# Second half's output projection moved 15 pairs into the first half's last FFN, with seven products behind it

## The chip, the cores and the metric

The kernel runs on one core of one Trainium2 chip. The metric is the device time of one execution in microseconds; the time given for a kernel is the median of several runs. A profile is one further execution, taken by the hardware profiler. The engines are called TensorE (PE; its weight loads PEld), VectorE (DVE), ScalarE (ACT), GpSimd (POOL) and SyncE (SP, which here issues nearly all transfers).

## The reference, cut to what matters

One layer of a hybrid decoder, 1024 channels wide, for a prompt of 1024 tokens and 8 single tokens that continue older sequences, all in float32:

```python
x = x + 0.5 * swiglu_ffn(rms_norm(x, ffn1_norm), w_gate1, w_up1, w_down1)   # first FFN, 2816 hidden
h = rms_norm(x, mix_norm);  proj = h @ w_in
ya = silu(layer_norm(causal_dwconv(glu(proj), width 31)))                   # mixer, group A
ys = grouped_rms_norm((ssd_scan(causal_dwconv(proj, width 4)) + D * xs) * silu(z))   # mixer, group B
x = x + concat([ya, ys]) @ w_out                                            # output projection
x = x + 0.5 * swiglu_ffn(rms_norm(x, ffn2_norm), w_gate2, w_up2, w_down2)   # last FFN
y = rms_norm(x, final_norm)
# swiglu_ffn(x) = (silu(x @ w_gate) * (x @ w_up)) @ w_down
```

The outputs are `y` for the prompt and the 8 tokens, and the new states of the two convolutions and of the scan.

## The kernel before

**Halves.** The tokens are cut in two: half 0 has the first 512 prompt tokens and the 8 single ones (520 columns, in two blocks of 260), half 1 the other 512. Activations lie with channels on the partitions, as 8 tiles per 1024 channels. State `sa` belongs to half 0, `sb` to half 1.

**Precision.** Every float32 operand is split in `hi` (rounded by a ScalarE copy) and `lo` (the rest, by a VectorE subtraction); weights likewise in `wh`/`wl` from the raw tile `wr`. A product is three matmuls: `wh` by `hi`, `wh` by `lo`, `wl` by `hi` (`mm3`, L348).

**Units.** TensorE's work is a list `prog` of units (`Unit`, L50), each one weight tile and its matmuls; on half 0 each matmul has 260 columns, on half 1 512. A *pair* is one of the 22 hidden tiles of an FFN: `gate(f)` and `up(f)`, 48 matmuls each on half 0. `down(gi, d)` multiplies the hidden tiles of group `gi` into output tile `d`: 3 matmuls per hidden tile and block. `GROUPS` (6, 5, 5, 6) and `GROUPS7` (3, 4, 4, 4, 3, 4) say how the 22 are grouped.

**Seven products.** `sevens()` computes a pair in seven smaller products, as Strassen's scheme in the Winograd form does with a 2 x 2 split: 7 x 12 matmuls of half the tokens (260 columns on half 0, 256 on half 1) in place of gate and up. Its weights are sums of quarter tiles (`ws`, four VectorE instructions per pair), each split by ScalarE and VectorE (`ww`), and its activations sums of token halves (`t12`, `t34`), made by `norm7` together with the norm. Before the change the first FFN of half 0 (`f1a`) has 3 plain pairs and 19 in seven products, the last FFN of half 0 (`f2a`) 22 plain pairs, the last FFN of half 1 (`f2b`) 22 in seven products, and the first FFN of half 1 (`f1b`) 22 plain pairs. With `hold` some last groups' downs are kept until all products are done.

**Order.** The program on TensorE is: `f1a`; four units of `f1b`; input projection of half 0; rest of `f1b`, under which half 0's mixer runs on VectorE, ScalarE and partly TensorE; output projection of half 0 (16 units); input projection of half 1; `f2a`, under which half 1's mixer runs; output projection of half 1 (`wout_units`, after all 22 pairs); the last 8 downs of `f2a`, under which `late_norm_b` makes half 1's statistics, norm and sums; `f2b`. The final norm of half 0 (`final_task`) is started after the last down of `f2a` has been issued.

**Planner.** The order of VectorE's and ScalarE's instructions is worked out when the kernel is built. Side work (mixer, norms) is written as generators in `Runner`, and a model clock with a price per instruction (`cost_t` for TensorE, L191) says when an operand will be ready; a step is emitted when its engine can take it. Urgent tasks go first. Evictions (`post`) are emitted with their unit. If a unit is not `ready`, the clock is moved on in steps of 0.1 us and side work is emitted until it is. Each engine runs its own instructions in the order in which they were emitted; transfers go through SP's queue in order too. Work tiles come from one pool of 70 slots.

**Rows of x.** `rms_task` stores the residual rows in DRAM (`xsp`) and `reload` brings them back when the next stage adds to them. Half 1's rows after its output projection stay in SBUF (`sb.x`) until the last FFN adds to them.

Of the kernel before, what the change touches and what calls it, by code (L numbers as in the profile page):

```python
# [5 lines left out]
F32 = mybir.dt.float32  # L6
# [184 lines left out]
def cost_t(op, aps, k):  # L191
    if op == "transpose":
        return 0.11
    n = size(aps[0])
    if aps[1].dtype == F32R:
        return 0.003 + 0.000417 * n
    return 0.00167 * max(n, 128) * (0.64 if aps[1].shape[-1] == HD else 1.0)


# [5 lines left out]
def body(tc, xt0, xt1, vec, tri, eye, hexp, wgu1, wgu2,  # L205
# [124 lines left out]
    def split(t, h, n=None):  # L330
        n = n or NTOK[h]
        hi = slot(n, F32R, "hi")
        lo = slot(n, F32R, "lo")
        S.activation(out=hi, in_=t[:, :n], func=AF.Copy)
        clk.defer(V, [t, hi], lo, lambda: V.tensor_tensor(out=lo, in0=t[:, :n], in1=hi.bitcast(F32), op=ALU.subtract))
        return hi, lo
# [82 lines left out]
    def rms_task(st, h, gname, spill=None):  # L419

        rs = slot(NTOK[h], nm="rs")
        yield from rstd_task(st.acc, NTOK[h], D_, rs)
        yield from norm_task(st, h, gname, rs, spill)

    def norm_task(st, h, gname, rs, spill=None):
        n = NTOK[h]
        hn = []
        last = None
        for k in range(KT + 1):
            if k < KT:  # L430
                yield need(V, st.x[k], rs)
                t = slot(n, nm="hn")
                V.scalar_tensor_tensor(out=t, in0=st.x[k][:, :n], scalar=vv(gname, k), in1=rs, op0=ALU.mult, op1=ALU.mult)
                if spill:
                    store(spill[k], st.x[k][:, :n])
                st.x[k] = None
            if last is not None:
# [5 lines left out]
    def norm7(st, h, gname, rs, whole):  # L443


        n = NTOK[h]
        m = n // 2
        st.hn7, st.read, tt = [None] * KT, [], []
        for k in range(KT // 2):
            ts = []  # L450
            for j in (k, k + KT // 2):
                yield need(V, st.x[j], rs)
                t = slot(n, nm="hn")
                V.scalar_tensor_tensor(out=t, in0=st.x[j][:, :n], scalar=vv(gname, j), in1=rs, op0=ALU.mult, op1=ALU.mult)
                st.read.append(j)
                yield need(S, t)
                st.hn7[j] = split(t, h, n if whole or j > k else m)
                ts.append(t)
            up, dn = ts
            a, b = slot(n, nm="t12"), slot(n, nm="t34")  # L460
            yield need(V, up, dn)
            V.tensor_tensor(out=a[:, :m], in0=up[:, m:], in1=up[:, :m], op=ALU.subtract)
            V.tensor_tensor(out=b[:, :m], in0=dn[:, m:], in1=up[:, m:], op=ALU.subtract)
            yield need(V, a)
            V.tensor_tensor(out=a[:, m:], in0=dn[:, m:], in1=a[:, :m], op=ALU.subtract)
            yield need(V, a)
            V.tensor_tensor(out=b[:, m:], in0=dn[:, :m], in1=a[:, m:], op=ALU.subtract)
            both = []
            for t in (a, b):
                yield need(S, t)  # L470
                both.append(split(t, h))
            tt.append(both)
            del ts, up, dn, a, b, t
        st.tt = tt

    def reload(st, h, src, d):
# [9 lines left out]
    def always():  # L486
        return True

    def ffn_units(h, st, wgu, wd, late_norm=False, rows=None, last=None, plain=None, hold=1):


        groups = GROUPS if plain is None else GROUPS7
        starts = [sum(groups[:g]) for g in range(len(groups))]

        def ready():
# [206 lines left out]
        if plain is not None:  # L702
            for f in range(plain):
                out += [gate(f), up(f)]
                if f + 1 in starts:
                    out += [down(starts.index(f + 1) - 1, d) for k in range(KT // 2) for d in (k, k + KT // 2)]
            more, held = sevens()
            out += more
            st.seven_end = len(out)
            out += held  # L710
            if last:
                return out + [end(d, b) for b in range(2) for d in range(KT)]
            return out + [down(len(groups) - 1, d) for d in range(KT)]
# [122 lines left out]
        out += [zu(i) for i in range(KT)]  # L836
        return out

    def wout_units(h, st, mx):
        n = NTOK[h]  # L840
        cur = {}

        def unit(d, j):
            def go(w):
                if j == 0:
                    reload(st, h, xsp[h], d)
                cur["p"] = mmt(h)
# [426 lines left out]
    def mix_tasks(h, mx, other):  # L1274
# [155 lines left out]
    mx = [State(), State()]  # L1430
    for m in mx:
        m.u, m.xs, m.xn, m.z, m.dtT = [], [None] * 12, 0, 0, None
        m.dt_done = m.ssd_done = m.sample_done = m.gate_done = m.ya_ready = m.ys_ready = False
# [12 lines left out]
    def late_norm_b():  # L1446
        rs = slot(NTOK[1], nm="rs")
        yield from rstd_task(sb.acc, NTOK[1], D_, rs)
        yield from norm7(sb, 1, "ffn2_norm", rs, False)

    def start_norm(st, h, g):
        return act(lambda: run.add([rms_task(st, h, g, spill=xsp[h])], True))

    def first_stat_b():

# [28 lines left out]
    prog += [start_norm(sa, 0, "ffn2_norm"), act(lambda: run.add(mix_tasks(1, mx[1], sa)))] + win_units(1, sb, mx[1])  # L1484
    prog += f2a[:-8] + wout_units(1, sb, mx[1])
    prog += [act(lambda: run.add([late_norm_b()], True))] + f2a[-8:]
    prog += [act(lambda: run.add([final_task(sa, sa.acc, yt0, 0, NTOK[0])]))] + f2b
    units = [u for u in prog if isinstance(u, Unit)]

    with tc.manual_schedule():  # L1490
# [37 lines left out]
        def first_norm():  # L1528
            yield from rstd_task(sa.acc, n, D_, sa.rs)
            sa.late = False  # L1530
            yield from constants()
            yield from norm7(sa, 0, "ffn1_norm", sa.rs, False)
        run.add([first_norm()], True)
        i, made = 0, 1
        for u in prog:
# [44 lines left out]
SLOTS = 70  # L1580
LEAD = 4
STAT_B = 80
RAWS = 4
TAIL = 256
SAMPLE_LATE = True
# [90 lines left out]
```

## Time and profile before

| | |
|---|---|
| median of 3 runs | 2196.7 us (2195.86 to 2197.72) |
| the profiled execution | 2199.06 us, of which 2197.3 are the span from the first to the last instruction |
| mean granted TensorE clock | 0.989 |
| TensorE busy | 2148.5 us, 14711 matmuls |
| VectorE busy | 1710.4 us |
| ScalarE busy | 947.9 us |
| moved by DMA | 255.17 MB |

The profiled execution's own time is 2.4 us above the median of the runs. Times inside the trace are microseconds from the start of the span. In tile names the number of the buffer is left out, so `mm<-hi,ww` is every matmul of a seven-product pair's rounded parts. All instructions bear the line of one helper (L162), so work is told apart by its tiles. A number in square brackets is the idle time of the engine in front of the instruction and what ended it. Matmuls are pipelined, so the time of one is longer than the step from one to the next.

### The profile page before, as it was taken

To read this page: it belongs to the slowest core of one execution; us is meant where nothing else is said; L and a number is where in the kernel's file an instruction comes from. 1 tells how busy PE (TensorE), PEld (TensorE's weight loads), DVE (VectorE), ACT (ScalarE), POOL (GpSimd) and SP (SyncE) were. 2 spreads that over 40 slices of the span, in tenths; PEclk is the share of its full clock that TensorE was granted. 3 is DMA by queue.
4 is the path that set the end of the run, shared out by engine and by line. 5 is a ranking of instruction groups with operands and counts; after the bars stand their busy time and mean duration, and the time that the engine had idled before them with its cause. 6 is when DMAs were issued, how large, how long until landed. Compare 5 with 4: busy or idle time off the path is not lost.

```text
span 2197.3 us, 36877 instructions
## 1 busy us (share of the span) xinstructions
PE 2148.5 (98%) x14711; PEld 1974.9 (90%) x14711; DVE 1710.4 (78%) x3010; ACT 947.9 (43%) x1679; POOL 2.4 (0%) x24
## 2 busy tenths in 40 slices
PE   8999999999999999999999999999999997999997
PEld 7899999999987788889987889999999897899997
DVE  7877788699999899966489998988534368777776
ACT  5544454424556422453233556533423234544452
POOL 0000000000000000000000000000000000000000
PEclk9999999999999999999999999999999998999998
DMA  4323334423344455425243553442233323333322
GB/s 133 95 97 125 103 108 141 149 79 105 102 154 152 124 171 180 154 77 183 89 134 81 96 161 118 129 149 87 82 110 114 103 82 101 90 114 96 105 90 81
DMA packets 107987, 255.17 MB, mean 116 GB/s; under 512 B 14312, under 2 KB 30600, under 8 KB 107816
## 3 DMA queue, kind: packets, MB, share of 16 engines
q1 hardware_dynamic: 107240, 252.30, 38.0%
q8 instruction: 115, 1.88, 0.3%
q10 hardware_dynamic: 576, 0.52, 0.1%
q14 instruction: 56, 0.46, 0.1%
HBM read 231.90 MB, written 20.88 MB: 115 GB/s over the span
## 4 chain that ended last, share of the span: by engine, by line
PE 76%; DVE 4%; DMA 0%; issue 0%; ACT 0%; DVEq 0%
PE mm L162 73%; PE aux L162 4%; DVE x L162 1%; DVE ws L162 1%; DVE ww L162 1%; DMA zr<-zsp 0%; DVE lo L162 0%; DVE wl L162 0%; DVE acc L162 0%; DVE t L162 0%; DVE xc L162 0%; DVE ra L162 0%; DVE hn L162 0%; DVE ya L162 0%; DVE ry L162 0%
## 5 line engine op out<-in xcount | busy, mean ns | idle before, releaser
L162 PE MATMUL mm<-hi,wh 128*128 128x260 f32 (+2 forms) x3146 | 862.0, 326 | 7.1 <-ACT wh L162 6.5
L162 PE MATMUL mm<-lo,wh 128*128 128x260 f32 (+2 forms) x3146 | 850.7, 322 | 2.6 <-DVE lo L162 2.3
L162 PE MATMUL mm<-hi,wl 128*128 128x260 f32 (+2 forms) x3146 | 849.1, 322 | 0.5 <-DVE wl L162 0.5
L162 PEld LDWEIGHTS mm<-hi,wh 128*128 128x128 f32 x3146 | 526.7, 189 | 60.1 <-ACT wh L162 6.5
L162 PEld LDWEIGHTS mm<-lo,wh 128*128 128x128 f32 x3146 | 525.1, 189 | 51.5 <-DVE lo L162 4.6
L162 PEld LDWEIGHTS mm<-hi,wl 128*128 128x128 f32 x3146 | 525.1, 189 | 48.3 <-DVE wl L162 0.7
L162 DVE TENSOR_TENSOR wl<-wr,wh 128x1024 fp32r<-128x1024 f32 (+4 forms) x359 | 359.7, 1004 | 126.1 <-ACT wh L162 124.8
L162 PE MATMUL mm<-hi,ww 128*128 128x256 f32 (+1 forms) x2296 | 425.6, 285 | 13.2 <-ACT hi L162 7.9
L162 ACT ACTIVATE wh<-wr 128x1024 fp32r<-128x1024 f32 (+4 forms) x359 | 314.5, 877 | 198.2 <-PE mm L162 147.4
L162 PEld LDWEIGHTS mm<-hi,ww 128*128 128x128 f32 x2296 | 361.0, 191 | 17.4 <-ACT hi L162 9.0
L162 DVE SCALAR_TENSOR_TENSOR ya<-u,vc,ya 128x512 f32<-128x512 f32 x480 | 336.1, 744 | 0.7 <-ACT ya L162 0.7
L162 PE MATMUL mm<-lo,ww 128*128 128x256 f32 (+1 forms) x1148 | 326.7, 285 | 3.2 <-DVE lo L162 3.1
L162 PEld LDWEIGHTS mm<-lo,ww 128*128 128x128 f32 x1148 | 219.5, 191 | 5.1 <-DVE lo L162 4.3
L162 ACT ACTIVATE hi<-sg 128x520 fp32r<-128x520 f32 (+1 forms) x88 | 55.9, 635 | 282.6 <-DVE sg L162 279.8
L162 ACT ACTIVATE ww<-ws 128x512 fp32r<-128x512 f32 x164 | 102.0, 622 | 40.8 <-DVE ws L162 40.8
L162 DVE TENSOR_TENSOR ww<-ws,ww 128x512 fp32r<-128x512 f32 x164 | 109.5, 683 | 11.7 <-ACT ww L162 11.3
L162 DVE SCALAR_TENSOR_TENSOR x<-mm,x 128x260 f32<-128x260 f32 (+2 forms) x160 | 83.4, 540 | 44.6 <-PE mm L162 44.2
L162 DVE TENSOR_TENSOR sg<-sg,mm 128x260 f32<-128x260 f32 (+2 forms) x113 | 51.1, 471 | 73.3 <-PE mm L162 72.6
L162 ACT ACTIVATE ww<-wr 128x512 fp32r<-128x512 f32 x123 | 76.9, 626 | 50.8 <-PE mm L162 24.1
L162 DVE TENSOR_TENSOR lo<-sg,hi 128x520 fp32r<-128x520 f32 (+1 forms) x88 | 60.9, 692 | 34.0 <-ACT hi L162 33.6
L162 ACT ACTIVATE q<-x 128x520 f32<-128x520 f32 (+2 forms) x63 | 36.8, 585 | 114.8 <-DVE x L162 113.5
L162 DVE TENSOR_TENSOR ww<-wr,ww 128x512 fp32r<-128x512 f32 x123 | 82.5, 682 | 1.2 <-ACT ww L162 1.1
(173 smaller groups left out, 1763.8 us busy)
## 6 DMA issues: line engine op xcount, KB each, us to landing
wr<-wgu SPq DMA_DIRECT2D x175, 512.0 KB, 3.9
wr<-win SPq DMA_DIRECT2D x72, 512.0 KB, 3.9
wr<-wd SPq DMA_DIRECT2D x64, 256.0 KB, 2.7
wr<-wout SPq DMA_DIRECT2D x32, 512.0 KB, 3.8
wr<-wd SPq DMA_DIRECT2D x32, 384.0 KB, 3.2
wr<-wd SPq DMA_DIRECT2D x32, 320.0 KB, 3.0
acsb<-acsd SPq DMA_DIRECT2D x32, 256.0 KB, 4.2
wr<-wd SPq DMA_DIRECT2D x32, 192.0 KB, 2.3
```

The source lines that it names most:

```text
L162: return f(*a, **k)
```

## The change

- `f1a` computes 4 pairs plainly instead of 3, in groups `GROUPS1A` (4, 3, 4, 4, 3, 4).
- `f2a` computes 15 pairs plainly and 7 in seven products, in groups `GROUPS2A` (5, 5, 5, 4, 3); the downs of the last two groups (16 units) are held to its end.
- The output projection of half 1 comes after the 15 plain pairs and the downs of their three groups. The mixer's last step (`mx.room`) waits for that place instead of for the end of `f2a`'s pairs.
- The norm of `f2a` also stores its normalized rows in DRAM (`nsp`); `sums7`, started in the middle of the output projection, loads them again and makes the sums that seven products need.
- The output projection stores half 1's rows in DRAM (`xsp2`) and lets go of them. Half 1's statistics (`stat_b`) run beside the seven products of `f2a`; its `norm7`, started with the held downs, loads the rows (`pairs`, two pairs ahead), and `f2b` loads them once more to add to them.
- The planner's price of a matmul goes from 0.003 + 0.000417 n to 0.005 + 0.000442 n us for n columns.

```diff
@@ cost_t
     if aps[1].dtype == F32R:
-        return 0.003 + 0.000417 * n
+        return 0.005 + 0.000442 * n
@@ norm_task
+                if keep:
+                    store(keep[k], t)
...
         st.hn = hn
+        if keep:
+            st.hn7 = hn
@@ new: sums (cut out of norm7), pairs, sums7
+    def pairs(h, src):
+        got = []
+        for k in range(KT // 2 + 2):
+            if k < KT // 2:
+                got.append([])
+                for j in (k, k + KT // 2):
+                    t = slot(NTOK[h], nm="x")
+                    D.dma_start(out=t, in_=src[j])
+                    got[-1].append(t)
+                del t
+            if k > 1:
+                yield got.pop(0)
+    def sums7(st, h, src):
+        tt = []
+        load = pairs(h, src)
+        for k in range(KT // 2):
+            yield from sums(*next(load), h, tt)
+        st.tt = tt
@@ norm7
+        load = pairs(h, src) if src else None
         for k in range(KT // 2):
+            xs = next(load) if src else (st.x[k], st.x[k + KT // 2])
...
@@ ffn_units
-                if f + 1 in starts:
-                    out += [down(starts.index(f + 1) - 1, d) for k in range(KT // 2) for d in (k, k + KT // 2)]
+                for gi in range(len(groups)):
+                    if f == min(starts[gi] + groups[gi], plain - 1) and starts[gi] + groups[gi] <= plain:
+                        out += [down(gi, d) for d in (NORMED if late_norm and gi == 0 else range(KT))]
+            st.plain_end = len(out)
@@ wout_units
+                    if out is not None:
+                        store(out[d], st.x[d])
+                        st.x[d] = None
@@ mix_tasks
-            yield lambda: other.ffns > h and mx.ya_ready
+            yield lambda: (mx.room if h else other.ffns > 0) and mx.ya_ready
@@ the program
-    f1a = ffn_units(0, sa, wgu1, wd1, late_norm=True, plain=GROUPS7[0], hold=2)
+    f1a = ffn_units(0, sa, wgu1, wd1, late_norm=True, plain=GROUPS1A[0], hold=2, groups=GROUPS1A)
-    f2a = ffn_units(0, sa, wgu2, wd2, rows=xsp[0])
-    f2b = ffn_units(1, sb, wgu2, wd2, plain=0,
+    f2a = ffn_units(0, sa, wgu2, wd2, rows=xsp[0], plain=PLAIN2A, hold=2, groups=GROUPS2A)
+    f2b = ffn_units(1, sb, wgu2, wd2, rows=xsp2, plain=0, groups=GROUPS7,
...
-    prog += f2a[:-8] + wout_units(1, sb, mx[1])
-    prog += [act(lambda: run.add([late_norm_b()], True))] + f2a[-8:]
+    wob = wout_units(1, sb, mx[1], xsp2)
+    prog += f2a[:sa.plain_end] + [act(room)] + wob[:KT] + [act(lambda: run.add([sums7(sa, 0, nsp)], True))] + wob[KT:]
+    prog += [act(lambda: run.add([stat_b()]))] + f2a[sa.plain_end:sa.seven_end]
+    prog += [act(lambda: run.add([norm7(sb, 1, "ffn2_norm", sb.rs, xsp2)], True))] + f2a[sa.seven_end:]
```

## Rows read from the trace of the kernel before

**Rows 1.** The page, first part: busy time, share and instructions of each engine.

```profile
PE 2148.5 (98%) x14711; PEld 1974.9 (90%) x14711; DVE 1710.4 (78%) x3010; ACT 947.9 (43%) x1679; POOL 2.4 (0%) x24
```

In the next group a row gives: from and to, length; busy time and count of PE, PEld, DVE, ACT, POOL; granted clock (1.00 is 2.4 GHz, 0.50 is 1.2 GHz); DMA share; GB/s. The stretches are, in order: entry to `f1a`'s seven products; four pairs of `f1a` without downs; `f1a`'s held downs; `f2a` up to its 2160th matmul; output projection of half 1; last downs of `f2a`; start of `f2b`; a pair of `f2b` with two downs of three; a pair of `f2b` alone.

**Rows 2.** Busy time of each engine in nine stretches.

```profile
67.62:84.50 16.88, 11.43 (x62) 10.42 (x61) 15.54 (x30) 7.59 (x16) 0.00 (x0) 0.70 0.16 36
301.25:341.56 40.31, 40.31 (x339) 40.31 (x338) 35.22 (x67) 22.40 (x46) 0.00 (x0) 1.00 0.32 101
345.22:385.44 40.22, 40.22 (x339) 40.22 (x338) 34.66 (x70) 18.73 (x32) 0.50 (x4) 1.00 0.42 133
1306.58:1601.33 294.75, 294.03 (x2463) 287.08 (x2462) 234.38 (x418) 140.48 (x249) 0.00 (x0) 1.00 0.39 117
1687.78:1776.77 88.99, 88.99 (x385) 72.04 (x385) 39.69 (x48) 24.77 (x32) 0.00 (x0) 1.00 0.34 104
1776.77:1821.64 44.87, 38.59 (x318) 38.33 (x316) 38.30 (x90) 18.24 (x32) 0.00 (x0) 0.94 0.21 68
1821.64:1837.20 15.56, 9.92 (x42) 8.74 (x43) 15.56 (x30) 6.49 (x14) 0.00 (x0) 0.52 0.30 102
1873.56:1888.37 14.81, 14.35 (x104) 13.38 (x103) 11.55 (x22) 7.11 (x14) 0.00 (x0) 1.00 0.32 97
1949.71:1959.67 9.96, 9.96 (x85) 9.95 (x84) 7.42 (x14) 4.83 (x10) 0.00 (x0) 1.00 0.46 132
```

**Rows 3.** Timeline of PE at the start of the last FFN.

```profile
1815.12 1.29 PE L162 MATMUL aux<-ones,acc 128*128 128x1 f32 x10 [2.23 <-DVE acc L162]
...
1820.47 1.31 PE L162 MATMUL aux<-ident,ry 128*128 128x128 f32 x6 [4.06 <-DVE ry L162]
...
1831.81 0.58 PE L162 MATMUL mm<-hi,ww 128*128 128x256 f32 x1 [2.23 <-ACT hi L162]
```

**Rows 4.** Timeline of DVE, same place: start, length, instruction, tiles, shapes, count.

```profile
1787.96 0.74 DVE L162 SCALAR_TENSOR_TENSOR hn<-x,vc,rs 128x512 f32<-128x512 f32 x1
...
1817.96 0.15 DVE L162 TENSOR_SCALAR rv<-aux 128x5 f32<-128x5 f32 x1
...
1827.39 2.09 DVE L162 SCALAR_TENSOR_TENSOR x<-x,vc,rs 128x520 f32<-128x520 f32 x3
...
1833.96 0.68 DVE L162 TENSOR_TENSOR lo<-t,hi 128x512 fp32r<-128x512 f32 x1
```

**Rows 5.** Timeline of PE and DVE at the first FFN's start.

```profile
51.16 0.50 PE L162 MATMUL aux<-hi,wh 128*128 128x260 f32 x2 [0.83 <-ACT hi L162]
...
77.18 1.31 DVE L162 TENSOR_TENSOR lo<-t,hi 128x520 fp32r<-128x520 f32 x2 [0.24 <-ACT hi L162]
...
77.20 0.58 PE L162 MATMUL mm<-hi,ww 128*128 128x260 f32 x1 [2.74 <-ACT hi L162]
```

The next view gives after the count: busy us, mean ns of one | idle us before them and what ended most of it.

**Rows 6.** Groups of instructions by form, VectorE, whole span.

```profile
L162 DVE TENSOR_TENSOR wl<-wr,wh 128x1024 fp32r<-128x1024 f32 x197 | 240.6, 1222 | 86.5 <-ACT wh L162 85.7
...
L162 DVE TENSOR_TENSOR ww<-ws,ww 128x512 fp32r<-128x512 f32 x164 | 109.5, 683 | 11.7 <-ACT ww L162 11.3
...
L162 DVE SCALAR_TENSOR_TENSOR x<-aux,x 128x260 f32<-128x260 f32 x88 | 33.3, 419 | 8.9 <-PE aux L162 8.9
...
L162 DVE TENSOR_TENSOR wl<-wr,wh 128x768 fp32r<-128x768 f32 x32 | 30.4, 951 | 4.7 <-ACT wh L162 4.3
...
L162 DVE TENSOR_TENSOR wl<-wr,wh 128x384 fp32r<-128x384 f32 x32 | 17.6, 551 | 2.9 <-ACT wh L162 2.8
```

**Rows 7.** Timeline of DVE, end of half 1's mixer.

```profile
1559.60 0.68 DVE L162 TENSOR_TENSOR lo<-ya,hi 128x512 fp32r<-128x512 f32 x1
```

**Rows 8.** Waits of PE, 187 to 212: in total, times, longest us.

```profile
PE aux L162 <- ACT hi L162: 1.8, 1, 1.8
PE mm L162 <- DVE ww L162: 1.1, 2, 0.6
```

**Rows 9.** Waits of SP's own queue, whole span: in total, times, longest us.

```profile
SPq L162 <- DVE wl L162: 988.2, 238, 10.1
```

**Rows 10.** Timeline of PE in a pair of the last FFN.

```profile
1891.99 0.50 PE L162 MATMUL mm<-hi,ww 128*128 128x256 f32 x2 [0.46 <-DVE ww L162]
```

More of the change, by code (lines that the diff above doesn't have):

```diff
@@ L28 @@
 GROUPS7 = (3, 4, 4, 4, 3, 4)
+GROUPS1A = (4, 3, 4, 4, 3, 4)
+GROUPS2A = (5, 5, 5, 4, 3)
 SLOT = 552
+NORMED = (0, 4, 1, 5, 2, 6, 3, 7)
 NCH = 4
@@ L324, in body @@
     xsp = [dr.tile([KT, P, NTOK[h]], F32, name=f"xsp{h}") for h in range(2)]
+    nsp = dr.tile([KT, P, NTOK[0]], F32, name="nsp")
+    xsp2 = dr.tile([KT, P, NTOK[1]], F32, name="xsp2")
     zsp = [dr.tile([KT, P, NTOK[h]], F32, name=f"zsp{h}") for h in range(2)]
@@ L417, in add_sq, with rms_task, norm_task @@
         clk.defer(V, [q], acc, lambda: V.tensor_tensor(out=acc, in0=acc, in1=q, op=ALU.add))
-    def rms_task(st, h, gname, spill=None):
+    def rms_task(st, h, gname, spill=None, keep=None):
         rs = slot(NTOK[h], nm="rs")
         yield from rstd_task(st.acc, NTOK[h], D_, rs)
-        yield from norm_task(st, h, gname, rs, spill)
-    def norm_task(st, h, gname, rs, spill=None):
+        yield from norm_task(st, h, gname, rs, spill, keep)
+    def norm_task(st, h, gname, rs, spill=None, keep=None):
         n = NTOK[h]
@@ L441, in norm_task, with sums @@
         st.hn = hn
-    def norm7(st, h, gname, rs, whole):
+        if keep:
+            st.hn7 = hn
+    def sums(up, dn, h, tt):
         n = NTOK[h]
         m = n // 2
-        st.hn7, st.read, tt = [None] * KT, [], []
+        a, b = slot(n, nm="t12"), slot(n, nm="t34")
+        yield need(V, up, dn)
+        V.tensor_tensor(out=a[:, :m], in0=up[:, m:], in1=up[:, :m], op=ALU.subtract)
+        V.tensor_tensor(out=b[:, :m], in0=dn[:, m:], in1=up[:, m:], op=ALU.subtract)
+        yield need(V, a)
+        V.tensor_tensor(out=a[:, m:], in0=dn[:, m:], in1=a[:, :m], op=ALU.subtract)
+        yield need(V, a)
+        V.tensor_tensor(out=b[:, m:], in0=dn[:, :m], in1=a[:, m:], op=ALU.subtract)
+        del up, dn
+        both = []
+        for t in (a, b):
+            yield need(S, t)
+            both.append(split(t, h))
+        tt.append(both)
@@ new lines, in pairs, with norm7 @@
+    def pairs(h, src):
[10 more added lines that the diff above has]
+                yield got.pop(0)
+    def norm7(st, h, gname, rs, src=None):
+        n = NTOK[h]
+        hn7, st.read, tt = [None] * KT, [], []
+        load = pairs(h, src) if src else None
@@ L449, in norm7 @@
         for k in range(KT // 2):
+            xs = next(load) if src else (st.x[k], st.x[k + KT // 2])
             ts = []
-            for j in (k, k + KT // 2):
-                yield need(V, st.x[j], rs)
+            for i, j in enumerate((k, k + KT // 2)):
+                yield need(V, xs[i], rs)
                 t = slot(n, nm="hn")
-                V.scalar_tensor_tensor(out=t, in0=st.x[j][:, :n], scalar=vv(gname, j), in1=rs, op0=ALU.mult, op1=ALU.mult)
+                V.scalar_tensor_tensor(out=t, in0=xs[i][:, :n], scalar=vv(gname, j), in1=rs, op0=ALU.mult, op1=ALU.mult)
@@ L455, in norm7 @@
                 st.read.append(j)
                 yield need(S, t)
-                st.hn7[j] = split(t, h, n if whole or j > k else m)
+                hn7[j] = split(t, h, n if j > k else n // 2)
                 ts.append(t)
[L459 to L473, printed above, removed]
+            del xs
+            yield from sums(*ts, h, tt)
+            del ts, t
@@ L474, in norm7 @@
+        st.hn7, st.tt = hn7, tt
+    def sums7(st, h, src):
[3 more added lines that the diff above has]
+            yield from sums(*next(load), h, tt)
         st.tt = tt
@@ L487, in always, with ffn_units @@
         return True
-    def ffn_units(h, st, wgu, wd, late_norm=False, rows=None, last=None, plain=None, hold=1):
-        groups = GROUPS if plain is None else GROUPS7
+    def ffn_units(h, st, wgu, wd, late_norm=False, rows=None, last=None, plain=None, hold=1, groups=GROUPS):
         starts = [sum(groups[:g]) for g in range(len(groups))]
@@ L837, in win_units, with wout_units @@
         return out
-    def wout_units(h, st, mx):
+    def wout_units(h, st, mx, out=None):
         n = NTOK[h]
@@ L1432, in body @@
         m.u, m.xs, m.xn, m.z, m.dtT = [], [None] * 12, 0, 0, None
-        m.dt_done = m.ssd_done = m.sample_done = m.gate_done = m.ya_ready = m.ys_ready = False
+        m.dt_done = m.ssd_done = m.sample_done = m.gate_done = m.ya_ready = m.ys_ready = m.room = False
     run = Runner()
@@ L1437, in act, with stat_b, room, start_norm @@
         return ("act", fn)
-    f1a = ffn_units(0, sa, wgu1, wd1, late_norm=True, plain=GROUPS7[0], hold=2)
+    f1a = ffn_units(0, sa, wgu1, wd1, late_norm=True, plain=GROUPS1A[0], hold=2, groups=GROUPS1A)
     f1b = ffn_units(1, sb, wgu1, wd1, rows=xt1)
     end_a = sa.seven_end
-    f2a = ffn_units(0, sa, wgu2, wd2, rows=xsp[0])
-    f2b = ffn_units(1, sb, wgu2, wd2, plain=0,
+    f2a = ffn_units(0, sa, wgu2, wd2, rows=xsp[0], plain=PLAIN2A, hold=2, groups=GROUPS2A)
+    f2b = ffn_units(1, sb, wgu2, wd2, rows=xsp2, plain=0, groups=GROUPS7,
                     last=lambda c, m: run.add([final_task(sb, sb.acc, yt1, c, m)]))
[L1446 to L1452, printed above, removed]
+    def stat_b():
+        sb.rs = slot(NTOK[1], nm="rs")
+        yield from rstd_task(sb.acc, NTOK[1], D_, sb.rs)
+    def room():
+        mx[1].room = True
+    def start_norm(st, h, g, keep=None):
+        return act(lambda: run.add([rms_task(st, h, g, spill=xsp[h], keep=keep)], True))
     def first_stat_b():
@@ L1483, in body @@
     prog += [start_norm(sb, 1, "mix_norm")] + wout_units(0, sa, mx[0])
-    prog += [start_norm(sa, 0, "ffn2_norm"), act(lambda: run.add(mix_tasks(1, mx[1], sa)))] + win_units(1, sb, mx[1])
-    prog += f2a[:-8] + wout_units(1, sb, mx[1])
-    prog += [act(lambda: run.add([late_norm_b()], True))] + f2a[-8:]
+    prog += [start_norm(sa, 0, "ffn2_norm", nsp), act(lambda: run.add(mix_tasks(1, mx[1], sa)))]
+    prog += win_units(1, sb, mx[1])
+    wob = wout_units(1, sb, mx[1], xsp2)
+    prog += f2a[:sa.plain_end] + [act(room)] + wob[:KT] + [act(lambda: run.add([sums7(sa, 0, nsp)], True))] + wob[KT:]
+    prog += [act(lambda: run.add([stat_b()]))] + f2a[sa.plain_end:sa.seven_end]
+    prog += [act(lambda: run.add([norm7(sb, 1, "ffn2_norm", sb.rs, xsp2)], True))] + f2a[sa.seven_end:]
     prog += [act(lambda: run.add([final_task(sa, sa.acc, yt0, 0, NTOK[0])]))] + f2b
@@ L1531, in first_norm @@
             yield from constants()
-            yield from norm7(sa, 0, "ffn1_norm", sa.rs, False)
+            yield from norm7(sa, 0, "ffn1_norm", sa.rs)
         run.add([first_norm()], True)
@@ L1582 @@
 STAT_B = 80
+PLAIN2A = 15
 RAWS = 4
```

## The prediction

> **What bounds the kernel now.** I read the page first: TensorE is busy for nearly the whole span and VectorE for three quarters [rows 1]. So what counts is the columns that TensorE streams and the few places where it stands. Next I cut the span into stretches by the order of the work units (every unit has a known number of matmuls) and asked for the busy time of each [rows 2]. Where TensorE streams undisturbed, a 260-column matmul costs 40.31 us / 336 = 0.120 us; this is first-FFN work in seven products with no down products among it, and VectorE is busy for 35.2 of the 40.3 us. The 512-column ones of the output projection cost 88.99 / 384 = 0.2317 us.
>
> Against these prices two stretches lose much. At the entry to the first FFN's seven products (67.62 to 84.50), 60 matmuls take 16.88 us instead of 7.2: 9.7 lost. At the seam from the first half's last down products to the second half's last FFN, 288 matmuls take 44.87 instead of 34.6 us, and the next 42 of 256 columns 15.56 instead of 5.0 (a later stretch of 84 takes 9.96): 10.3 + 10.6 = 20.9 lost. The granted clock says the same: 0.70 in the first, 0.94 and 0.52 in the second.
>
> The timeline tells why. At the seam TensorE runs out at 1812.89, stands 2.23 and 4.06 us in front of the first half's *final* norm (`acc`, `ry`), and then for `hi` and `lo` of the FFN norm [rows 3]. On VectorE that FFN norm (`norm7`) begins at 1787.96, because the statistics before it wait for the last projection product, and the last `lo<-t` ends at 1834.64; the final norm's eight `x<-x,vc,rs` and its chain of small instructions (from `rv` at 1817.96 until TensorE goes on at 1820.47, 2.5 us) stand in between [rows 3, 4]. So the norm is 1834.64 - 1812.89 = 21.8 us late. At the first entry it is the same work: the matmul at 77.20 waits for `hi`, and the last `lo<-t` pair ends at 78.49 [rows 5].
>
> **The change, step by step.**
>
> *Seven products for seven pairs.* A plain pair is 96 matmuls of 260 columns, a pair in seven products 7 x 12 = 84. Seven pairs: 84 fewer x 0.120 = **-10.1 us**. Each such pair asks VectorE for 7 `ww` and 4 `ws` of 0.68 us, five 260-column instructions of 0.42 and one `lo`, in place of two `wl` of 1.22 [rows 6], but the stretch without downs in rows 2 is this mixture, at full pace.
>
> *Fourth plain pair in the first FFN.* 12 matmuls more: **+1.4 us**. It brings one pair (96 x 0.120 = 11.5) and 8 down products of 24 instead of 18 matmuls (48 x 0.120 = 5.8) in front of the entry, 17.3 us of cover. VectorE gets two `wl` of 1024 (2 x 1.22), four instructions of 260 columns on the pair's result (4 x 0.42) and two of 520 (2 x 0.69), and eight `wl` of 512 instead of 384 (8 x 0.13): 6.6 us [rows 6]. That leaves 10.7 us. The norm is late by 78.49 - 67.62 less the 1.4 us of the product that needs no sums: 9.5 us. It just fits; of the 9.7 lost I leave 2: **-7.7 us**, between 0 and -9.7.
>
> *Output projection earlier.* The same 16 units run at the same price; only their place moves. It must not come before the mixer is done. 15 pairs and 24 down products of five are 15 x 96 + 24 x 30 = 2160 matmuls; the kernel before has streamed 2160 of this stage, with the same mixer beside them, at 1601.33 [rows 2], and the mixer's last `lo<-ya` ends at 1560.28 [rows 7]: 41 us in hand. 0.
>
> *Sums from DRAM.* `sums7` runs beside the second eight projection units, 8 x 24 x 0.2317 = 44.5 us. VectorE has there 8 evictions, 7 `acc` and 8 `lo` (0.69 each), 8 `wl` (1.22) and 16 half-width `t` (0.42): 32.4 us [rows 6]. It fits; for the first fill I take **+1**, between 0 and the 9.7 of the other entry.
>
> *The seam.* The statistics go out beside the seven products; `norm7` may start with the first held down product instead of 11.2 us after it. The held stretch becomes 16 down products, 8 x 24 + 8 x 18 = 336 matmuls, exactly those of the first FFN that took 40.22 us, against the 36.1 us up to 1812.89 now: 4.1 more. The final norm falls behind the FFN norm: 8 x 0.67 + 2.5 = 7.9 us off VectorE's queue. Against that stand 16 more evictions (6.7) and `wl` of 512 (as long as a `ww`) and 384 for those of 768 (9.9 - 7.6 = 2.3) [rows 6]. Late: 21.8 - 11.2 - 4.1 - 7.9 + 9.0 = 7.6 us. What is 21.8 late today loses 20.9, the slow clock included, so I take 8: **-12.9 us**, between 0 and -20.9. The FFN norm's first instruction now waits for a row from `xsp2`; behind it on VectorE stand the evictions and `wl` for which TensorE waits in turn.
>
> *The statistics among the products.* The like of it, at 190 to 205 in the first FFN, makes TensorE stand 1.8 us for `hi` and 1.1 for `ww` [rows 8]. **+3**, between 0 and 3.
>
> *Third group of downs straight after its pair.* Its last input is split late, as at 51.16, where TensorE waits 0.83 us for `hi` [rows 5]: **+1**, between 0 and 1. These downs may also use the mixer's four banks when two are free: 0, as the 41 us cover a mixer that waits for a bank.
>
> *More transfers.* Eight stores each to `nsp` and `xsp2`, 24 loads, and 8 more weight loads, all on SP's queue, about 10.6 MB more on some 255. `pairs` holds two pairs ahead, so I charge 0; but the weight loads on that queue already wait 988 us for `wl`, up to 10.1 at once [rows 9], and a row load behind one is late by as much. The bound is 10.1 us at the seam. The Trainium skill ("DMA: Bandwidth & Descriptors", section Anatomy of one DMA) says that a wait on a semaphore is served by the issuing sequencer before dispatch, so it holds up everything issued after it on that engine. The 988 us of waits on SP agree. By this rule alone the seam would lose 8 + 10 and the sum be some 10 us worse; that is part of rival B.
>
> *Planner's prices.* The plan took 0.003 + 0.000417 x 260 = 0.111 us for a matmul that takes 0.120; the new formula gives 0.1199, and 0.2313 for 512 columns. So the order of VectorE's and ScalarE's instructions changes everywhere. What can come back: in seven pairs of the last FFN each pair loses 14.81 - 9.96 - 18 x 0.2317 = 0.68 us on a late `ww` [rows 2, 10], 4.8 in all. What it can cost: as much again or more. I take 0, between -5 and +5.
>
> *Sum.* -10.1 + 1.4 - 7.7 + 1 - 12.9 + 3 + 1 = **-24.3 us**. The profiled execution has a span of 2197.3 and took 2199.06 with what lies around it, 2.4 above the median of the runs, so it would become 2174.8, and the median 2196.7 - 24.3 = **2172.4**.
>
> **The rivals.**
>
> *A, the forecast*, 2164 to 2180: 0.42.
>
> *B, the seam stays as it is.* 7.6 us late is enough for the final norm to be queued in front again (it is started as soon as the held products are issued), and rows that wait in DRAM can be held up on SP. For it: the narrow balance and the 988 us. Against: the statistics are gone from the chain. No gain there: 2172.4 + 12.9 = 2185.3. Chance 0.22.
>
> *C, the first entry stays late.* The margin is 1 us, and ScalarE's `hi` ended the wait. 2172.4 + 7.7 = 2180.1, and both B and C 2193.0. C alone 0.11, both 0.03.
>
> *D, the seven products don't pay in this place*, since VectorE sets the pace (the change doesn't do what it says). Against: 35.2 of 40.3 us. 2172.4 + 10.1 = 2182.5. Chance 0.05.
>
> *E, nothing is late*: the seam loses 2, the entry 0, the statistics are free, the `ww` waits gone: 2172.4 - 6 - 2 - 3 - 4.8 = 2156.6. Chance 0.12.
>
> *F, slower.* The plan at new prices puts `ww` late in every pair of seven products, not in seven. There are 18 + 7 + 22 = 47; 40 x 0.68 = 27 us more: 2199.6. It eats the gain from 24.3 / 40 = 0.61 us a pair. For it: the wait exists. Against: it is absent in the first FFN, where VectorE has the same work per pair. Chance 0.05, in 0.03 of which the new order costs still more elsewhere.
>
> **How the numbers follow.** A is the likeliest: 2172.4. E reaches down to 2156.6, and B with 5 us for the new order up to 2190: 2157 to 2190 leaves out F, B and C together and the tail of E, under 2 in 10. Measurement tells 0.2%, about 4.4 us. Slower means over 2201.1: F at its worst, and 0.02 for a loss that I don't see, 0.05. Within 0.2%: F at its size, and half of B and C together, which ends at the edge, 0.04. Faster: 0.91.
>
> **What would show it.** TensorE has 72 fewer matmuls of 260 columns (84 - 12). The entry to the first FFN's seven products shows a clock of 1.00 and no wait for `hi`. The projection begins without a wait. The seven pairs of the second FFN take 84 x 0.120 = 10.1 us each; more, with VectorE full, is D. At the seam the wait for `ry` of the final norm is gone and `hi`/`lo` cost under 10 us; the final norm's `x<-x,vc,rs` ahead of the last `lo<-t` is B. A wait for `ww` in every pair of the first FFN is F. What would make it wrong most: the order of VectorE's queue at the two entries, since both balances are within a few us of zero.

## The result and the profile after

The median is **2163.4 us** (2162.27 to 2163.72, four runs) against 2196.6 for the kernel before, run beside it: 33.3 us less, ratio 0.9847 (0.983 to 0.9864). Forecast were 2172.4 and a range of 2157 to 2190: the sign and the range held, and 9 us more came off than forecast. The profiled execution took 2163.27 us, 35.8 less than that of before, and its span is 35.8 shorter as well, so the two traces can be compared stretch by stretch.

The page's first part, as [rows 1]:

```profile
span 2161.5 us, 37044 instructions
...
PE 2128.3 (98%) x14639; PEld 1957.8 (91%) x14639; DVE 1753.3 (81%) x3133; ACT 962.3 (45%) x1730; POOL 2.4 (0%) x24
```

TensorE has 72 matmuls fewer, the 84 less 12 of the forecast. VectorE has 123 instructions and 42.9 us more.

Busy time by stretch, columns as in [rows 2]. In order: 60 matmuls at the entry to the first FFN's seven products; `f2a` up to its 2160th matmul; output projection of half 1; the seven pairs in seven products (588 matmuls); the 16 held downs (336); the first 36 matmuls of `f2b`; a pair of `f2b` with two downs of three.

```profile
83.80:91.01 7.21, 7.21 (x62) 7.21 (x61) 7.18 (x15) 4.60 (x9) 0.00 (x0) 1.00 0.21 73
1295.13:1589.05 293.92, 293.55 (x2463) 286.59 (x2462) 226.52 (x413) 137.16 (x247) 0.00 (x0) 1.00 0.39 121
1589.05:1678.34 89.29, 89.29 (x387) 72.11 (x385) 51.92 (x77) 29.39 (x41) 0.00 (x0) 1.00 0.45 151
1678.34:1751.12 72.78, 72.26 (x602) 72.05 (x601) 62.48 (x124) 40.59 (x83) 0.00 (x0) 1.00 0.31 101
1751.12:1800.78 49.66, 42.79 (x349) 42.37 (x347) 48.66 (x105) 23.94 (x45) 0.00 (x0) 0.94 0.45 135
1800.78:1807.55 6.77, 6.77 (x44) 6.77 (x45) 5.50 (x18) 2.30 (x5) 0.00 (x0) 0.71 0.01 4
1845.09:1859.18 14.09, 14.09 (x104) 13.29 (x103) 11.48 (x22) 7.23 (x15) 0.00 (x0) 1.00 0.45 141
```

At 0.120 us a matmul of 260 columns the entry loses nothing any more (60 x 0.120 = 7.2), the seven pairs lose 72.78 - 588 x 0.120 = 2.2 us, and the seam loses 49.66 - 336 x 0.120 = 9.3 in the held downs and 6.77 - 36 x 0.120 = 2.5 behind them: 11.8 where it was 20.9. The held downs of the seam are the one stretch left here with VectorE full (48.66 of 49.66) and TensorE not.

The timeline of VectorE shows the mixer's last step and then the seam; in brackets the idle time in front and what ended it:

```profile
1503.64 0.68 DVE L166 TENSOR_TENSOR lo<-ya,hi 128x512 fp32r<-128x512 f32 x1
...
1752.00 0.75 DVE L166 SCALAR_TENSOR_TENSOR hn<-x,vc,rs 128x512 f32<-128x512 f32 x1
...
1753.18 0.75 DVE L166 SCALAR_TENSOR_TENSOR hn<-x,vc,rs 128x512 f32<-128x512 f32 x1 [0.44 <-DMA x<-xsp]
...
1797.87 0.69 DVE L166 TENSOR_TENSOR acc<-acc,q 128x520 f32<-128x520 f32 x1
...
1800.95 0.17 DVE L166 TENSOR_SCALAR rv<-aux 128x5 f32<-128x5 f32 x1 [0.24 <-PE aux L166]
...
1803.25 0.69 DVE L166 TENSOR_TENSOR lo<-t,hi 128x512 fp32r<-128x512 f32 x1
```

TensorE's timeline and its waits (whole span: in total, times, longest):

```profile
1791.38 0.40 PE L166 MATMUL mm<-hi,wl 128*128 128x260 f32 x2
1798.62 2.29 PE L166 MATMUL aux<-ones,acc 128*128 128x1 f32 x10 [6.83 <-DVE acc L166]
```

```profile
PE aux L166 <- DVE acc L166: 9.2, 2, 6.8
...
PE mm L166 <- DVE pb L166: 1.6, 3, 0.6
```

The mixer is done at 1504.3, and the projection starts at 1589.05. The norm begins 0.9 us after the first held down, as it should, and its last `lo<-t` ends at 1803.94. TensorE ran out of products at 1791.79, so the norm is 12.1 us late (7.6 forecast), and TensorE spends 6.83 of that in front of the first half's *final* norm (its sum of squares, `acc`). No wait for `ww` is left in `f2b`; the kernel before had one in each of seven pairs, as in [rows 10]. SP's queue with the row loads of the seam:

```profile
1730.53 17.44 SPq L166 DMA_DIRECT2D wr<-wd  x5
1748.02 2.80 SPq L166 DMA_DIRECT2D x<-xsp  x6
...
1757.76 0.90 SPq L166 DMA_DIRECT2D x<-xsp  x2
```

Five weight loads with their waits hold the queue for 17.44 us, but the rows go out four microseconds ahead of their first use, and the whole exchange through DRAM (265.75 against 255.17 MB) shows one wait of VectorE at the seam, 0.44 us.

### The profile page after: what moved, and what is told of

It reads as the page before. It is cut to its first block, busy times and chain, and to the rows that moved or that the text cites. A ratio compares the mean times of both kernels' runs of the same rounds, so it can differ in the third digit from the quotient of the medians.

```text
span 2161.5 us, 37044 instructions
## 1 busy us (share of the span) xinstructions
PE 2128.3 (98%) x14639; PEld 1957.8 (91%) x14639; DVE 1753.3 (81%) x3133; ACT 962.3 (45%) x1730; POOL 2.4 (0%) x24
## 2 busy tenths in 40 slices
DMA packets 114902, 265.75 MB, mean 123 GB/s; under 512 B 15080, under 2 KB 32392, under 8 KB 114728
## 4 chain that ended last, share of the span: by engine, by line
PE 91%; DVE 7%; issue 1%; DMA 1%; ACT 1%; SPq 0%; DVEq 0%; ACTq 0%
PE mm L166 76%; PE aux L166 14%; DVE wl L166 1%; DVE x L166 1%; DVE acc L166 1%; DVE st L166 1%; DVE sw L166 1%; DMA zr<-zsp 1%; DVE xc L166 0%; DVE ya L166 0%; DVE syv L166 0%; DVE lo L166 0%; DMA x<-xt 0%; DVE sg L166 0%; DVE ra L166 0%
## 5 line engine op out<-in xcount | busy, mean ns | idle before, releaser
L166 PE MATMUL mm<-hi,wh 128*128 128x260 f32 (+2 forms) x2628 | 756.8, 334 | 7.2 <-ACT wh L166 6.5
L166 PE MATMUL mm<-lo,wh 128*128 128x260 f32 (+2 forms) x2628 | 745.4, 329 | 2.8 <-DVE lo L166 2.8
L166 PE MATMUL mm<-hi,wl 128*128 128x260 f32 (+2 forms) x2628 | 744.1, 329 | 0.5 <-DVE wl L166 0.5
L166 PEld LDWEIGHTS mm<-hi,wh 128*128 128x128 f32 x2628 | 445.3, 189 | 60.2 <-ACT wh L166 6.5
L166 PE MATMUL mm<-hi,ww 128*128 128x260 f32 (+1 forms) x2632 | 479.3, 282 | 2.2 <-DVE pb L166 1.6
L166 PE MATMUL mm<-lo,ww 128*128 128x260 f32 (+1 forms) x1316 | 371.7, 282 | 0.0
L166 DVE TENSOR_TENSOR ww<-ws,ww 128x512 fp32r<-128x512 f32 x188 | 126.2, 685 | 18.9 <-ACT ww L166 18.7
L166 PE MATMUL aux<-hi,wh 128*128 128x260 f32 x668 | 135.1, 283 | 0.0
L166 PE MATMUL aux<-lo,wh 128*128 128x260 f32 x668 | 134.6, 283 | 0.2 <-DVE lo L166 0.2
L166 PE MATMUL aux<-hi,wl 128*128 128x260 f32 x668 | 134.4, 283 | 0.2 <-DVE wl L166 0.2
L166 PEld LDWEIGHTS aux<-hi,wl 128*128 128x128 f32 x668 | 102.9, 188 | 0.6 <-DVE wl L166 0.6
```

The lines of the kernel that those rows point to most:

```text
L166: return f(*a, **k)
```

## The experiments

Each was timed beside the kernel before, whose median was 2198.5 us beside the first four, 2199.2 beside the next four, and 2198.9 beside the last four. Differences are to the kernel before timed with them, and differences to the change compare two such differences. Between timings the kernel before moved from 2196.6 to 2199.2, the changed kernel from 2163.4 to 2162.7; so differences to the change of 2 or 3 us are uncertain by as much unless their medians agree, and where it matters those are given too. Line numbers differ by a few between kernels.

### The planner's price alone

```diff
@@ cost_t, in the kernel before
-        return 0.003 + 0.000417 * n
+        return 0.005 + 0.000442 * n
```

> The kernel before with the planner's new price of a matmul and nothing else. Theory P (the new price took away TensorE's small waits: 7 x 0.7 us on a late ww in the last FFN, about 4 us around the statistics in the first FFN, some at the end, against 2 us more under the first mixer): about 8 us faster, 2188.5, with no wait for ww left in the last FFN. Rival R (those waits went because the work around them moved): 2196.6, the waits still there. Either way the entry to the first FFN's seven products and the seam before the last FFN stay late.

2198.5, ratio 0.9999 (0.999 to 1.0008): **0.0 us**. The waits for `ww` in `f2b` do go:

```profile
1885.10:1899.20 14.10, 14.10 (x104) 13.32 (x104) 11.47 (x22) 7.23 (x15) 0.00 (x0) 1.00 0.31 103
```

It is the pair that took 14.81 in [rows 2]. By stretch of the two traces, `f2b` to the end takes 10.1 us less, 2.9 of them in its first 36 matmuls at the seam. But `f2a` up to the projection takes 5.7 more under half 1's mixer (its plain pairs 3.6, its downs 2.2), `f1b` under half 0's mixer 2.3, the input projections 1.1, and the first FFN 0.2 more (its downs and plain pairs lose 1.9 more, its products 1.7 less). Half 1's mixer ends some 36 us earlier, at 1524.5 instead of 1560.3:

```profile
1522.00 2.49 DVE L162 TENSOR_TENSOR lo<-ya,hi 128x512 fp32r<-128x512 f32 x4
```

Gained are 10.1, lost 9.3: they nearly cancel, so neither theory had it: the waits went, and the time didn't. That the planner counts on a slower TensorE, and so lets more side work in ahead of the evictions, would fit the earlier mixer and its dearer stretch; that is argued from the code and not shown: only the effect is measured.

### The change at the old price

```diff
@@ cost_t, in the changed kernel
-        return 0.005 + 0.000442 * n
+        return 0.003 + 0.000417 * n
```

> The changed kernel with the planner's old price. Theory P: the 8 us come back, 2171.5, with 0.7 us waits for ww in pairs of the last FFN. Rival R: 2163.4, no such waits. A third way: the old price also makes the norm at the seam come later, then more than 8 us.

2171.0, ratio 0.9875 (0.9861 to 0.9888): -27.5. The changed kernel timed again gave -36.3 (below), so in the change the price is worth **8.8 us**; by the medians as they stand, 2171.0 against 2163.4 and 2162.7, it is 7.7 to 8.4. The waits for `ww` are back, seven of them in `f2b` and four in the first FFN:

```profile
PE mm L166 <- DVE ww L166: 4.5, 11, 0.5
```

```profile
1850.07:1864.95 14.88, 14.35 (x104) 13.34 (x104) 11.64 (x22) 7.12 (x14) 0.00 (x0) 1.00 0.44 133
```

The span is 8.0 us longer than the changed kernel's: `f2b` takes 4.7 more, the first FFN 2.9 more, and the held downs at the seam lose 12.0 instead of 9.3; `f1b` gets 2.1 back. Half 1's mixer ends 253.2 us after `f2a` starts, 41.2 ahead of the projection, which is the 41 us of the forecast; with the new price it is 209.2 and 85.

### The fourth plain pair alone

```diff
@@ in the kernel before
+GROUPS1A = (4, 3, 4, 4, 3, 4)
...
-    f1a = ffn_units(0, sa, wgu1, wd1, late_norm=True, plain=GROUPS7[0], hold=2)
+    f1a = ffn_units(0, sa, wgu1, wd1, late_norm=True, plain=GROUPS1A[0], hold=2, groups7=GROUPS1A)
```

> The kernel before with the fourth plain pair and the groups of the first half's first FFN only. Theory: 12 matmuls more (+1.4) and none of the 9.7 us at the entry lost any more, clock at full there: 8.2 us faster, 2188.4. Rival (the entry was cured by the new price, not by the cover): 1.4 us slower, 2198.0, with the wait for hi still there.

2186.6, ratio 0.9948 (0.9935 to 0.996): **-12.0**. The entry is clean:

```profile
83.90:91.20 7.30, 7.30 (x64) 7.30 (x63) 7.28 (x14) 4.51 (x9) 0.00 (x0) 1.00 0.22 72
```

By stretch: entry -9.65, the extra matmuls +1.44, the first down of `f1a` -0.8, the products up to half 1's first statistics -0.8, `f2a`'s plain pairs -1.4. The edit is worth more than its own place shows.

### The change with three plain pairs

```diff
-    f1a = ffn_units(0, sa, wgu1, wd1, late_norm=True, plain=GROUPS1A[0], hold=2, groups=GROUPS1A)
+    f1a = ffn_units(0, sa, wgu1, wd1, late_norm=True, plain=GROUPS7[0], hold=2, groups=GROUPS7)
```

> The changed kernel with three plain pairs in the first FFN as before. Theory: the entry is late again by about 9.5 us with a stretch at the lower clock, 1.4 us of matmuls fewer: 8 us slower, 2171.4. Rival (the new price cures the entry by itself): 1.4 us faster, 2162.

2181.0, ratio 0.9921 (0.9907 to 0.9934): -17.6, so inside the change the pair is worth **18.7 us** (17.6 to 18.3 by the medians). Two stretches of the first FFN, the entry and the one with half 1's first statistics:

```profile
68.00:84.40 16.40, 11.34 (x64) 10.33 (x63) 14.72 (x29) 7.54 (x15) 0.00 (x0) 0.69 0.16 41
187.80:208.00 20.20, 15.72 (x113) 14.90 (x112) 16.99 (x41) 10.66 (x20) 0.00 (x0) 0.92 0.29 97
```

The entry loses its 9 us again, at a clock of 0.69. The statistics lose 8.3 us; 6.4 in the kernel before, and 2.1 in the changed one. They are started at a fixed place in the list of units, and with four plain pairs another unit stands there. But that shift is not enough: with four pairs at the old price (the two experiments above) the statistics still lose 3.2, and four pairs ahead of them lose 2.5 more on a late `ww`. This is the wait of the change at the old price, between 92 and 186 us:

```profile
PE mm L166 <- DVE ww L166: 1.5, 4, 0.4
```

With the new price and three pairs it is 7.2 on the kernel before and 8.3 here. So only the pair and the price together bring it down to 2.1.

### 22 plain pairs in the last FFN of half 0

```diff
-    f2a = ffn_units(0, sa, wgu2, wd2, rows=xsp[0], plain=PLAIN2A, hold=2, groups=GROUPS2A)
+    f2a = ffn_units(0, sa, wgu2, wd2, rows=xsp[0], plain=PLAIN2A, hold=2, groups=GROUPS2A, tail=True)
...
-            more, held = sevens()
+            more, held = sevens() if not tail else (
+                [v for f in range(plain, NFT) for v in (gate(f), up(f))], [down(len(groups) - 2, d) for d in range(KT)])
```

The rest of the change stays; `sums7` and the rows in `nsp` are left out.

> The changed kernel with all 22 pairs of the first half's last FFN plain; the projection still after 15 pairs, the statistics among the other 7, the norm beside the held downs; no sums for this half. Theory (the 84 matmuls fewer are worth their 10.1 us, less some 2 us of waits that the seven products show): 8 us slower than the changed kernel, 2171.5. Rival D (the products gain nothing, VectorE sets their pace): 2163.4 or faster. The seam should lose the same 11 to 12 us as in the changed kernel.

2172.3, ratio 0.9877 (0.9864 to 0.9891): -26.9, so the products are worth **9.4 us** of the 10.1 that their matmuls cost (8.9 to 9.6 by the medians as they stand). The seam doesn't feel them:

```profile
1758.87:1808.54 49.67, 42.76 (x348) 42.35 (x347) 48.58 (x105) 24.15 (x45) 0.00 (x0) 0.95 0.35 107
```

### The first half's final norm started later

```diff
-    prog += [act(lambda: run.add([final_task(sa, sa.acc, yt0, 0, NTOK[0])]))] + f2b
+    prog += f2b[:LATER] + [act(lambda: run.add([final_task(sa, sa.acc, yt0, 0, NTOK[0])]))] + f2b[LATER:]
...
+LATER = 10
```

> The changed kernel with the first half's final norm started ten units into the last FFN instead of right in front of it. Theory H (at the seam TensorE stands 6.8 us in its own queue in front of the final norm's statistics, which nothing needs yet): 6 us faster, 2157.5, the seam loses 5 instead of 11.7. Rival N (the FFN norm's last sums end 12 us after TensorE ran out, so a wait for hi or lo takes the place): 0 to 2 us faster, 2162, waits for hi and lo at the first products.

2164.2, ratio 0.984 (0.9827 to 0.9854): -35.0, **no gain** over the change (by the medians 0.8 to 1.5 slower). The held downs run at full pace, and the time is lost behind them:

```profile
1750.33:1790.86 40.53, 40.49 (x338) 40.28 (x337) 39.61 (x89) 19.13 (x37) 0.00 (x0) 1.00 0.48 147
1790.86:1803.13 12.27, 6.77 (x39) 5.95 (x37) 12.08 (x22) 6.47 (x13) 0.00 (x0) 0.79 0.20 64
```

```profile
1799.98 0.58 PE L166 MATMUL mm<-lo,ww 128*128 128x256 f32 x1 [3.32 <-DVE lo L166]
```

TensorE now stands before the sums of the FFN norm instead of before the final norm: 9.1 us less are lost in the held downs and 9.7 more in the pairs of `f2b`. What it stands in front of is not the cause: VectorE, busy for 12.08 of the 12.27 us, has more to do at the seam than the cover is long.

### Statistics at the head of the norm

```diff
-    prog += [act(lambda: run.add([stat_b()]))] + f2a[sa.plain_end:sa.seven_end]
-    prog += [act(lambda: run.add([norm7(sb, 1, "ffn2_norm", sb.rs, xsp2)], True))] + f2a[sa.seven_end:]
+    prog += f2a[sa.plain_end:sa.seven_end]
+    prog += [act(lambda: run.add([stat_norm_b()], True))] + f2a[sa.seven_end:]
```

> The changed kernel with the second half's statistics at the head of its norm, beside the held downs, instead of among the seven products. Theory (11 us of the norm's lateness before came from the statistics): the norm begins some 5 to 10 us later and the seam loses as much more, 2168 to 2173; the 1.3 us at the first products of the first half disappear. Rival (the seam is a matter of VectorE's load alone): 2163 or a little faster.

2167.8, ratio 0.9856 (0.9842 to 0.9869): -31.4, **4.9 slower** than the change (4.5 to 5.1 by the medians). The norm starts 7.3 us later and the held downs take 54.51 instead of 49.66:

```profile
1759.31 0.75 DVE L166 SCALAR_TENSOR_TENSOR hn<-x,vc,rs 128x512 f32<-128x512 f32 x1
```

```profile
1750.85:1805.36 54.51, 45.29 (x367) 45.00 (x365) 50.50 (x125) 23.36 (x44) 0.00 (x0) 0.92 0.41 121
```

The 1.3 us at the first products of `f2a` come back, as they belong to the statistics there.

### Twelve plain pairs, ten in seven products

```diff
-GROUPS2A = (5, 5, 5, 4, 3)
+GROUPS2A = (4, 4, 4, 3, 4, 3)
-PLAIN2A = 15
+PLAIN2A = 12
```

> The changed kernel with 12 plain pairs and 10 in seven products in the first half's last FFN, in groups of 4, 4, 4, 3, 4, 3. The mixer's last part was ready 85 us before the projection, and this takes some 45 us of it. Theory: 36 matmuls fewer, 4.3 us faster, 2159. Rival (the mixer is not ready at the new place, or the slots run out): TensorE waits in front of the projection, 2165 or more.

2159.8, ratio 0.9821 (0.9807 to 0.9834): -39.3, **3.0 faster** than the change (2.8 to 3.5 by the medians; the same step on top of one held group, below, gives 3.7 within one timing). 36 matmuls fewer are 4.3 us; 2.2 are given back in the plain pairs under the mixer. The mixer still ends 27.6 us before the projection.

### One held group of seven pairs

```diff
-GROUPS2A = (5, 5, 5, 4, 3)
+GROUPS2A = (5, 5, 5, 7)
-    f2a = ffn_units(0, sa, wgu2, wd2, rows=xsp[0], plain=PLAIN2A, hold=2, groups=GROUPS2A)
+    f2a = ffn_units(0, sa, wgu2, wd2, rows=xsp[0], plain=PLAIN2A, hold=1, groups=GROUPS2A)
```

The same 336 matmuls at the seam, in 8 downs of 42 instead of 8 of 24 and 8 of 18, so half as many evictions and, in fewer and longer pieces, weight splits (`wl`) for VectorE.

> The changed kernel with the last seven pairs of the first half's last FFN in one held group of 7 instead of groups of 4 and 3: the same 336 matmuls of cover, but 8 down products fewer, so 16 evictions and some wl less on VectorE (about 6.9 us) beside the norm. Theory V (the seam loses what VectorE's load makes the norm late, 12 us): the norm is 5 us late, 6 to 7 us faster than the changed kernel, about 2157. Rival Q (the seam is lost in TensorE's queue in front of the final norm, whose sum of squares takes the same time): 0 to 2 us faster.

2155.6, ratio 0.9802 (0.9789 to 0.9815): -43.4, **7.1 faster** than the change. The held downs and what follows:

```profile
1750.45:1790.68 40.23, 40.23 (x339) 40.23 (x337) 39.39 (x77) 19.28 (x33) 0.00 (x0) 1.00 0.43 141
1790.68:1796.06 5.38, 5.38 (x48) 5.38 (x47) 4.46 (x12) 3.37 (x7) 0.00 (x0) 1.00 0.23 81
```

336 matmuls in 40.23 us are the full price, and the clock stays at 1.00. The final norm is started at the same place in the program. VectorE has 28 instructions fewer in the stretch (77 for 105, in 40.23 instead of 49.66 us) and ends its last `lo<-t` here:

```profile
1794.05 0.68 DVE L166 TENSOR_TENSOR lo<-t,hi 128x512 fp32r<-128x512 f32 x1
...
1795.25 0.16 DVE L166 TENSOR_SCALAR rv<-aux 128x5 f32<-128x5 f32 x1
```

That is 9.2 us earlier, and ahead of the final norm's `rv`. Against the change 9.4 us are won in the held downs and 1.4 in the 36 matmuls behind them; 3.8 are given back in the rest of `f2b`, for a cause that stays open.

### Both, and the final norm later on top

```diff
-GROUPS2A = (5, 5, 5, 4, 3)
+GROUPS2A = (4, 4, 4, 3, 7)
-PLAIN2A = 15
+PLAIN2A = 12
...
hold=1 for f2a, as above; the second kernel also with LATER = 10
```

> The same with 12 plain pairs and groups 4, 4, 4, 3, 7. Theory V: both gains add, 3 and 6 us, 2154. Rival Q: 2160, the gain of the pairs alone.

> The same, with the first half's final norm started ten units into the last FFN. It gained nothing while the FFN norm was 12 us late. Theory V: with that norm nearly in time TensorE's wait in front of the final norm's statistics is what is left, 2 to 5 us faster than without, 2150 to 2152. Rival: 2154 again, the wait for the FFN norm's lo takes the place again.

Both together: 2151.9, ratio 0.9785 (0.9772 to 0.9798), -47.1, **10.8 faster** than the change: the 3.0 and the 7.1 add up, and this version beats both kernels. With the final norm later: 2152.9, ratio 0.9788 (0.9775 to 0.98), -46.0, no gain again; the 2 to 5 us expected were not there to win, as the first 36 matmuls of `f2b` lose only 1.1 without it. The page of the first:

```profile
PE 2123.4 (99%) x14603; PEld 1953.2 (91%) x14603; DVE 1769.5 (82%) x3169; ACT 967.0 (45%) x1749; POOL 2.4 (0%) x24
```

### The change once more

> The changed kernel itself beside these three on one chip, as what they are compared with: 33 us faster than the kernel before, by every theory.

2162.7, ratio 0.9838 (0.9824 to 0.9851): -36.3. In the first comparison it was -33.3; the intervals overlap, and its own median moved by 0.7. All differences "to the change" above are taken from this -36.3.

## Why it came out 9 us better than forecast

By runs, the way from the kernel before to the change splits into the fourth plain pair (-12.0, forecast -6.3 with its matmuls), the move, the products and the seam at the old price (-15.5 more, to -27.5; forecast -18.0), and the new price (-8.8 more; forecast 0). By stretches of the two traces:

| step of the forecast | forecast | measured |
|---|---|---|
| seven products for seven pairs | -10.1 | -9.2 (-9.4 by the run with 22 plain pairs) |
| fourth plain pair, its matmuls | +1.4 | +1.4 |
| entry to the first FFN's products | -7.7 | -9.7 |
| output projection earlier | 0 | +0.3, no wait |
| sums from DRAM | +1 | +0.3, the same stretch |
| seam | -12.9 | -9.1 |
| statistics among the products | +3 | +1.3 |
| third group of downs | +1 | 0 |
| more transfers | 0 | 0.4, part of the seam |
| not in the sum: `ww` waits in `f2b` | 0 | -4.9 |
| not in the sum: stretch of the first FFN with half 1's statistics | 0 | -4.3 |
| not in the sum: first down of `f1a`; `f2a` up to the projection; end of `f2b`; `f1b` | 0 | -0.8, -0.8, -1.5, +2.1 |

The measured column, with the sums from DRAM in the projection's line and the transfers in the seam's, comes to -35.2 of the 35.8 between the traces. What the sum didn't have at all gave 10.2 us, and the seam 3.8 less than forecast, so the misses cancel in part.

**The step that was furthest off** is "I take 0, between -5 and +5" for the planner's prices. As a price for one edit alone it was right: on the kernel before it gives 0.0. In the change it gives 8.8 (7.7 to 8.4 by the medians), beyond the end of the range. The named part of it, the 4.8 us of `ww` waits, came as worked out. The losses that the forecast set against it are real too, but the change pays only one of them: `f1b` costs 2.1 to 2.3 more in both kernels, whereas `f2a` up to the projection takes 5.7 more on the kernel before and 0.5 *less* in the change. Two gains come only there: the first FFN takes 2.9 less, and the held downs lose 2.7 less, where the kernel before shows +0.2 and +0.1. For the first FFN the four `ww` waits and the statistics are its place. Why the same price does so differently in `f2a` and at the seam, the runs don't settle; the downs are other ones (24 downs of five behind other pairs, against groups of 6, 5 and 5), and the mixer ends at another unit.

**Mis-sized by its neighbours** was the fourth plain pair. "Of the 9.7 lost I leave 2" was too careful: the cover was enough, and all 9.7 came back. What the forecast didn't have is what the pair does further on. The loss at half 1's first statistics falls from 6.4 to 2.1 us in the change, for which pair and price are both needed (5.6 with the pair alone, its `ww` waits included), and the pair is worth 12.0 alone and 18.7 in the change.

**The seam** was right in kind and 3.8 us too good. The norm began when it should. In "Late: 21.8 - 11.2 - 4.1 - 7.9 + 9.0" the 7.9 came only in part: the final norm's eight `x<-x,vc,rs` did fall behind the FFN norm (the first starts at 1809.21), its chain of small instructions did not, for `rv<-aux` stands at 1800.95, ahead of the last `lo<-t` at 1803.25. That is half the sight that the forecast named for rival B, and the 6.83 us in front of `acc` are its wait. But the final norm is not what costs the time. With it out of the way the time stays (2164.2, and 2152.9 beside 2151.9); with half as many evictions beside the same 336 matmuls 7.1 us go. The term that was too small is the + 9.0, what the 16 held downs ask of VectorE, which is busy for 48.66 of 49.66 us. From the first `hn` to the last `lo<-t` VectorE now runs all 32 evictions of the held downs and 14 of their 16 `wl`, where before it ran 12 of 16 and 4 of 8: some 13 us more at their recorded lengths (an estimate), because the norm now starts with the first held down.

**Rival C** is out (entry at 1.00), **D** is out (products worth 9.4 of 10.1), **F** is out: no pair of seven products waits for `ww` in the change. **E**, the entry and the `ww` waits free, was nearest of the rivals to what happened outside the seam.

**Moved to the front at no cost**, as forecast: the projection. The 41 us in hand were 41.2 at the old price. The Trainium skill ("DMA: Bandwidth & Descriptors", section Anatomy of one DMA) was set against the transfers: it says that a wait on a semaphore happens on the issuing sequencer, before dispatch. The forecast read from it that such a wait holds up what that sequencer issues next. By that reading alone the seam would have lost 10 us more. In this trace such a wait is there, 17.44 us for five weight loads; but it ended at 1748, four microseconds before the rows were wanted, and the seam lost 0.44 us to them. So the trace agrees that the queue was held up, and not that rows came late.

## What to carry to other kernels

If a late norm at a seam leaves VectorE full and TensorE standing, take work off VectorE in the cover (fewer, longer accumulations there: -7.1 us for the same matmuls) before moving what TensorE happens to wait for (no gain, twice). A setting that reorders everything, as a planner's price, can be worth nothing alone and some 8 us beside another change, so it is to be measured with and without the rest. And two edits can win a stretch that neither names and of which neither alone wins much: compare every stretch of the two traces, here 4.3 us of 35.8 at the first statistics.

## What the runs showed of the hardware

A stand of TensorE cost more than its own length. After it stood 6.83 us in the held downs, the first 18 matmuls of `f2b` waited for nothing and still came 0.213 us apart, where later ones of 256 columns come 0.118 apart. The granted clock of that stretch is 0.50, the lower of its two levels, 1.2 GHz:

```profile
1800.78:1804.55 3.77, 3.77 (x19) 3.77 (x19) 2.60 (x13) 0.83 (x2) 0.00 (x0) 0.50 0.00 0
```

The first 36 so take 6.77 us instead of 4.3 (granted clock 0.71 in all). At the two spacings some 1.9 us of the difference are the clock's (an estimate); the rest are six matmuls of the final norm in between. With one held group there is no stand at this place, the clock stays at 1.00, and the 48 records after the downs take 5.38 us.
